# Moving weight splits, bank copies and the steps of a norm's root around the start of two feed-forward blocks

## The chip, the core and the metric

The program runs on one core of a Trainium2 chip. TensorE (PE) multiplies matrices and writes into PSUM, which has eight banks of 128 partitions by 512 fp32 numbers. VectorE (DVE) and ScalarE (ACT) do the work on elements, and SyncE (SP) issues nearly all the transfers. Each engine takes its own instructions in the order in which they stand and waits for the others on semaphores. The metric is the device time of one execution in microseconds (us); lower is better.

## The reference, cut to what matters

Two groups of tokens (512 and 256, held side by side as 768 columns) go through two layers. Each layer has a token mixer, a feed-forward block with squared ReLU, and a gated embedding that is added; a norm with its own gain stands ahead of each.

```python
def rms_norm(x, g):
    xf = x.astype(jnp.float32)
    y = xf * lax.rsqrt(jnp.mean(xf * xf, axis=-1, keepdims=True) + EPS)
    return (y * g.astype(jnp.float32)).astype(x.dtype)
...
        h = rms_norm(x, norm_mlp[i])
        x = x + jnp.square(jax.nn.relu(h @ mlp_w_up[i])) @ mlp_w_down[i]
        gate = jax.nn.sigmoid(rms_norm(x, norm_ple[i]) @ ple_w_gate[i])
        x = x + (p[i] @ ple_w_proj[i]) * gate
```

The model width is 1024, the width inside the feed-forward block is 4096, and everything is fp32.

## The kernel before

Features lie on the partitions and tokens along the free axis, so an activation of the whole model is eight tiles of 128x768. An fp32 product is made of three products of rounded parts: an operand is split into hi (ACT copies it with rounding) and lo (DVE subtracts hi from the source), and PE adds hi·hi, hi·lo and lo·hi. In a row, the split of a weight tile reads `whi<-wraw` or `zhi<-wraw` on ACT and `wlo` or `zlo` on DVE. The tiles of tag w have two buffers; those of tag z have one, so a `zhi` cannot be written before PE has read the last one for the last time.

A norm is applied late. The tiles that PE reads are x times the gain, without the root. The sum of squares `acc` is made beside it, split into `ah` and `al` (`acc_parts`), summed over partitions on PE with a matrix of ones (`ss`, four matmuls), and turned into the root in the three steps of `rstd_steps`: `logs` (a table load on ACT, `v` on DVE from both halves of ss, `ln` on ACT, each half behind its v, then `y` = exp), `newton` (a square on ACT, again called `ln`, and a new `v` on DVE), and `result` (the root `rstd`, on DVE). Only the evacuation of a product (`rectified`, rows `y<-p,rstd_mlp`) needs the root.

The feed-forward block has 16 chunks of 256 hidden features. Chunks 0 and 1 are plain (`up_plain`): 96 matmuls of 128x384, eight blocks of the input times three parts times two halves of the output (p1, p2) times two halves of the tokens (sides). Their weights are two raw tiles, the "direct" one, split into zhi and zlo, and the "second" one, split into whi and wlo. Later chunks use Strassen's seven products, for which the input has to be combined: for each of four pairs of blocks, `norm.combine` makes two scaled copies on ACT (`q`, `q`), two sums on DVE, a rounded `t` on ACT, two more sums, a second `t`, and two subtractions on DVE. I call these eleven steps a combination. Work tiles such as `q`, `v`, `ln` and `y` take six buffers in turn, so the second q of the third combination takes the buffer that `v` holds until the root is made.

In the first layer (layer 0) `ahead` runs before the block: it multiplies the second half of the projected input embedding in four products of 12 matmuls (`pj`, two banks each), copies the banks out on ACT (`pjs`) and stores them by SP, and makes the norm's root and the first two combinations beside it. Chunk 0 then knows its root (`known`) and makes the third and fourth combination. In layer 1 the first two combinations are made earlier, in the product ahead, and chunk 0 does not know its root: it makes the sum of squares, the root and the last two combinations while it multiplies. There its 96 matmuls come in four groups of 36, 36, 12 and 12 (n = 0 to 3).

PSUM is divided by tags: A has four banks, B and C two each. Inside `manual_schedule` the order on PE, ACT and DVE is the order in which the code is written, so a call that stands later in the code stands later in the engine's queue. `weave` takes one step of each list in turn.

Of the kernel before, what the change touches and what calls it, by code (L numbers as in the profile page):

```python
# [47 lines left out]
def trunk_kernel(ctx: ExitStack, tc: tile.TileContext, a: dict, out: bass.AP):  # L48
# [67 lines left out]
    def both(name="mm", tag=None):  # L116

        return [t[:, :H] for t in fresh(name, 2, tag)]
# [52 lines left out]
    class Norm:  # L171
# [30 lines left out]

        aside = temp

        def acc_parts(self):
            ah, al = self.aside("ah", F32R), self.aside("al", F32R)
            self.last = split(ah, al, self.acc)
            return ah, al

        def sum_squares(self, psum, also=None, parts=None, tag=None):  # L210

# [22 lines left out]
        def rstd_steps(self, psum, ss=None):  # L234
            n = self.n
            if ss is None:
                ss = self.sum_squares(psum)
            v, ln, y = (self.aside(name) for name in ("v", "ln", "y"))

            def logs():  # L240
                with tc.issue_after(self.last):
                    act.preload_act_table_set(EXP_LN)
                for t, o, e in ss:
                    dve.tensor_scalar(v[:, o:e], t, 1.0 / D, EPS, ALU.mult, ALU.add)  # L244
                for t, o, e in ss:
                    act.activation(ln[:, o:e], t, AF.Ln, scale=1.0 / D, bias=eps[:])  # L246
                act.activation(y, ln, AF.Exp, scale=-0.5)  # L247


            def newton():  # L250
                act.activation(ln, y, AF.Square)  # L251
                dve.scalar_tensor_tensor(v, ln, -0.5, v, ALU.mult, ALU.mult)  # L252

            def result():
                if self.rplace is None:
                    self.r = stat.tile([P, n], F32, tag="rstd", name=f"rstd_{self.name}")[:]
                else:
                    self.r = slot(self.rplace, f"rstd_{self.name}", F32)[:, :n]
                dve.scalar_tensor_tensor(self.r, v, 1.5, y, ALU.add, ALU.mult)  # L259

            return [logs, newton, result]
# [564 lines left out]
    def weave(*chains):  # L826

        for steps in itertools.zip_longest(*chains):
            for step in steps:
                if step:  # L830
                    step()
# [20 lines left out]
    def second_inputs(places):  # L852


        part = [], []
        ws = []

        def behind(i):
            if i < 2:
                raw = fetch(a["p"][1, :, i, :])  # L860
                hi, lo = (slot(places[2 * i + p], "p1") for p in range(2))
                split(hi[:], lo[:], raw[:, :T])
                part[0].append(hi[:])
                part[1].append(lo[:])
            elif i == 3:
                ws.append(weight(a["proj"][1, 1], 2))
            elif i == 5:
                ws.append(up_chunk(0, 0))
            elif i == 7:
                ws[1].split("second")  # L870

        def product(m):
            ps = both("pj", "AB"[m % 2])
            group2(ps, terms_of(ws[0], part, col=m * P))
            return ps

        return behind, product, ws

    def ahead(norm, product, w, places):


        ps = []

        def copied(m):
            t = slot(places[m], "pjs", F32)
            for f, o, e in pieces(ps[m]):
                act.activation(t[:, o:e], f, AF.Copy)
            nc.sync.dma_start(pj[1][KB // 2 + m], t[:])

        for m in range(KB // 2):  # L890
            ps.append(product(m))
            if m == 0:
                w.split("direct")
                parts = norm.acc_parts()
            else:
                copied(m - 1)
            if m == 2:
                weave(norm.combine(0))
        ss = norm.sum_squares(psum, parts=parts, tag="C")
        copied(m)  # L900
        weave(norm.rstd_steps(psum, ss), norm.combine(1))
        return norm.r

    def mlp(l, norm, nxt, w, places, early, product=None):
# [3 lines left out]
        r = None  # L908
# [7 lines left out]
        def squared(t):  # L916
            act.activation(t[:], t[:], AF.Square)  # L917
# [30 lines left out]
        def up_plain(u, w, make, then):  # L948
# [7 lines left out]
            def rects(*which):  # L956
                for i, o in which:
                    rectified((y1, y2)[i], ps[i][o], H * o, H * o + H, ALU.max)
# [5 lines left out]
            for n, (i, ks, sides) in enumerate(order):  # L964
                for k in range(*ks):
                    m, h = PAIRED[k] % (KB // 2), PAIRED[k] // (KB // 2)
                    c = slice(P * m, P * m + P)
                    hi, lo = w.w[f"w{i + 1}{h + 1}"]
                    for j, (wt, part) in enumerate(((hi, 0), (hi, 1), (lo, 0))):
                        for o in sides:  # L970
                            pe.matmul(
                                ps[i][o],
                                lhsT=wt[:, c],
                                rhs=xs[f"x{h + 1}{1 + o}"][m][part],
                                start=k == 0 and j == 0,
                                stop=k == KB - 1 and j == 2,
                            )
                if n == 0:
                    v = make()
                    split2 = [lambda: v.split("second")] if v.plain else []  # L980
                    todo1 = norm.combine(todo.pop(0)) if todo else []
                    rest, pend[:] = pend[:4], pend[4:]
                    if not known:
                        parts = norm.acc_parts()
                    weave(rest, todo1, split2)
                elif n == 1:
                    sums = [] if v.plain else [v.sums32, v.sums14, lambda: v.split("direct")]
                    weave(norm.combine(todo.pop(0)) if todo else [], sums, pend)
                    pend.clear()
                    if not known:  # L990
                        ss = norm.sum_squares(psum, parts=parts, tag="C")
                elif n == 2:
                    weave([lambda: v.split("direct" if v.plain else "s32")], [] if known else norm.rstd_steps(psum, ss))
                    r = norm.r
                    if known:
                        y1, y2 = big("y1"), big("y2")
                        rects((0, 1), (1, 1))
                else:
                    if not known:
                        y1, y2 = big("y1"), big("y2")  # L1000
                        rects((0, 1), (1, 1))
                    rects((0, 0))
                    squared(y1)
                    rects((1, 0))
                    pend.extend(acts_of(u, y1, y2, y2))
            return v
# [299 lines left out]
    for i, m in enumerate(PAIRED):  # L1306
        if i == 1:
            w += [weight(a["w_o0"][3], 4)] * 2
        ps = both()
# [103 lines left out]
```

## Time and profile before

| what | value |
|---|---|
| median of 3 runs | 1717.86 us (1717.43 to 1718.11) |
| the profiled execution | 1720.3 us, of which the span from first to last instruction is 1718.5 us |
| granted TensorE clock over the span | 0.991 |
| busy in the span | PE 97%, DVE 78%, ACT 50% |
| start of layer 0's feed-forward block | pj products 308.6 to 321.2 us, chunk 0 from 321.95, chunk 1 from 344.5, third chunk from 363.5 |
| start of layer 1's feed-forward block | chunk 0 from 1148.2 us, chunk 1 from 1165.7, third chunk from 1182.5 |

All times in rows are counted from the start of the span. A row of the timeline gives the start, the time from the start of the first to the end of the last instruction that it merges, the engine, the line, the operation, out<-in, the shape, the count, and in brackets the idle time of the engine before it with what ended that. The profiled execution's own time is its span and 1.8 us around it.

### The profile page before, as it was taken

Reading aid. Unit: us, or ns where it says so; the run is one execution under the profiler, and the core shown is the slowest. Engines: PE = TensorE matmul, PEld = TensorE weight load, DVE = VectorE, ACT = ScalarE, POOL = GpSimd, SP = SyncE. Lnnn points to the kernel's source line nnn. Section 1 sums busy time; section 2 is a strip of 40 time slices with the busy share of each in tenths; the row PEclk is TensorE's granted clock in tenths of the full one; section 3 lists DMA queues with packets and bytes.
Section 4 is the critical chain, followed back from the end, with each engine's and each line's share of the span. In section 5 each row is a group of like instructions: output and inputs, shape, how many; then the busy total and the mean of one; then the engine's idle time right before and its main releaser. Section 6 shows DMA issues by size and latency. Waiting matters only on the chain. (4 is left out here: it accounts for less than half of the span.)

```text
span 1718.5 us, 24204 instructions
## 1 busy us (share of the span) xinstructions
PE 1675.4 (97%) x9542; PEld 1617.8 (94%) x9542; DVE 1346.7 (78%) x2207; ACT 860.1 (50%) x1370; POOL 2.0 (0%) x30
## 2 busy tenths in 40 slices
PE   8999999899999999999999999999999999999996
PEld 7887788899999999999999999999999999999986
DVE  6588888889999989977765444668989999999676
ACT  6367756754454455544541111445455545555454
POOL 0000000000000000000000000000000000000000
PEclk9999999999999999999999999999999999999998
DMA  8753322211222222222321111211222222222222
GB/s 258 192 138 115 104 80 80 74 59 65 74 74 73 70 71 71 74 83 81 110 71 62 62 62 62 74 62 43 73 72 72 74 72 76 63 73 86 74 89 96
DMA packets 47842, 144.59 MB, mean 84 GB/s; under 512 B 6080, under 2 KB 10688, under 8 KB 47728
## 3 DMA queue, kind: packets, MB, share of 16 engines
q1 hardware_dynamic: 45168, 139.89, 25.8%
q10 hardware_dynamic: 2560, 3.15, 0.7%
q8 instruction: 75, 1.23, 0.3%
q14 instruction: 39, 0.32, 0.1%
HBM read 123.10 MB, written 10.48 MB: 78 GB/s over the span
## 5 line engine op out<-in xcount | busy, mean ns | idle before, releaser
L83 ACT ACTIVATE whi<-wraw 128x1024 fp32r<-128x1024 f32 (+2 forms) x73 | 75.5, 1034 | 185.6 <-PE b L129 53.0
L409 ACT ACTIVATE whi<-sum 128x1024 fp32r<-128x1024 f32 x56 | 59.0, 1053 | 146.6 <-PE a L441 146.6
L917 ACT ACTIVATE y<-y 128x768 f32<-128x768 f32 x64 | 53.5, 840 | 141.2 <-DVE y L914 141.2
L441 PE MATMUL a<-act,whi 128*128 128x384 f32 x448 | 96.7, 337 | 0.0
L84 DVE TENSOR_TENSOR wlo<-wraw,whi 128x1024 fp32r<-128x1024 f32 (+2 forms) x73 | 87.0, 1192 | 10.5 <-ACT whi L83 10.2
L441 PE MATMUL a<-t,zhi 128*128 128x384 f32 x448 | 92.2, 337 | 1.9 <-ACT c L1023 1.9
L441 PE MATMUL b<-t,zhi 128*128 128x384 f32 x448 | 92.0, 337 | 0.0
L441 PE MATMUL a<-t,whi 128*128 128x384 f32 x448 | 91.9, 337 | 0.0
L441 PE MATMUL a<-xs,whi 128*128 128x384 f32 x448 | 87.6, 337 | 0.8 <-DVE y L1046 0.8
L1079 DVE TENSOR_TENSOR x<-x,a 128x384 f32<-128x384 f32 x112 | 60.8, 553 | 33.7 <-PE a L441 33.5
L138 PE MATMUL mm<-xs_mix,whi 128*128 128x512 f32 (+1 forms) x320 | 82.9, 342 | 0.0
L441 PEld LDWEIGHTS a<-t,zhi 128*128 128x128 f32 x448 | 79.2, 188 | 2.2 <-ACT c L1023 2.2
L441 PEld LDWEIGHTS a<-xs,whi 128*128 128x128 f32 x448 | 79.0, 188 | 1.2 <-DVE y L1046 1.2
L441 PEld LDWEIGHTS a<-act,whi 128*128 128x128 f32 x448 | 79.8, 188 | 0.0
L441 PEld LDWEIGHTS b<-t,zhi 128*128 128x128 f32 x448 | 79.5, 188 | 0.0
L441 PEld LDWEIGHTS a<-t,whi 128*128 128x128 f32 x448 | 79.0, 188 | 0.0
L420 DVE TENSOR_TENSOR wlo<-sum,whi 128x1024 fp32r<-128x1024 f32 x56 | 68.5, 1223 | 9.6 <-ACT whi L409 9.6
L420 DVE TENSOR_TENSOR wlo<-wraw,whi 128x1024 fp32r<-128x1024 f32 x60 | 73.2, 1220 | 0.4 <-ACT whi L409 0.4
L409 ACT ACTIVATE zhi<-sum 128x1024 fp32r<-128x1024 f32 x56 | 59.3, 1060 | 20.9 <-DVE sum L385 16.5
L420 DVE TENSOR_TENSOR zlo<-sum,zhi 128x1024 fp32r<-128x1024 f32 x56 | 68.2, 1217 | 1.9 <-ACT zhi L409 1.9
L409 ACT ACTIVATE whi<-wraw 128x1024 fp32r<-128x1024 f32 x60 | 63.2, 1054 | 11.0 <-PE C L441 6.3
L330 ACT ACTIVATE t<-y 128x768 fp32r<-128x768 f32 x56 | 47.2, 843 | 41.1 <-DVE y L321 30.8
(290 smaller groups left out, 4639.2 us busy)
## 6 DMA issues: line engine op xcount, KB each, us to landing
wraw<-in_up SPq DMA_DIRECT2D x64, 512.0 KB, 3.5
wraw<-in_down SPq DMA_DIRECT2D x64, 512.0 KB, 3.5
wraw<-in_w_in SPq DMA_DIRECT2D x24, 512.0 KB, 3.4
wraw<-in_gate SPq DMA_DIRECT2D x16, 512.0 KB, 3.5
pj<-pjs SPq DMA_DIRECT2D x16, 384.0 KB, 3.6
wraw<-in_w_q SPq DMA_DIRECT2D x8, 512.0 KB, 4.8
wraw<-in_w_out SPq DMA_DIRECT2D x8, 512.0 KB, 3.5
x_in<-in_x SPq DMA_DIRECT2D x8, 384.0 KB, 7.1
```

What stands on the lines that cost most here:

```text
L83: first = act.activation(hi, src, AF.Copy)
L84: dve.tensor_tensor(lo, src, hi.bitcast(F32), ALU.subtract)
L138: pe.matmul(ps[:, o:e], lhsT=w, rhs=x[:, o:e], start=i == 0 and j == 0, stop=i == n - 1 and j == 2,)
L330: act.activation(t[0][:], (self.q1, self.q2)[i][:], AF.Copy)
L409: act.activation(hi[:], src, AF.Copy)
L420: dve.tensor_tensor(lo[:], src, hi[:].bitcast(F32), ALU.subtract)
L441: pe.matmul(ps, lhsT=a, rhs=b, start=start and i == 0, stop=i == len(terms) - 1, skip_group_check=True)
L917: act.activation(t[:], t[:], AF.Square)
L1079: dve.tensor_tensor(t[:, o : o + H], t[:, o : o + H], f, op)
```

## The change

The diff does four things.

1. In `ahead` the four products of the projected inputs take banks A, B, C, A in place of A, B, A, B, and ss takes B in place of C. The copy of a product is written behind the next product, as before, but `acc_parts` has moved from product 0 to behind copy 0, so that copy 0 stands ahead of `ah` and all the others behind it. The direct split of chunk 0 is written ahead of the products.
2. The table load becomes a step of its own (`table`), written right behind `acc_parts`.
3. In `ahead`, `logs` now stands ahead of the second combination, and `newton` and `result` behind it. In `up_plain` of a chunk that does not know its root, ss goes from n = 1 to n = 0, `logs` to the start of n = 1, `newton` and `result` to its end, behind the last combination, and the early scaled copies of the third combination go behind `acc_parts`.
4. The "direct" split of chunk 1's weights goes from n = 2, behind both combinations, to n = 1 between them where the root is known (layer 0). Where it is not known (layer 1) it stays at n = 2, ahead of which the whole root now stands. There, at the end of chunk 0, the evacuation of one half goes behind the square of y1.

On ACT in layer 0, from `ah` to the second combination. Before:

```order
L83 ACTIVATE ah<-acc_mlp_3328 128x768
L887 ACTIVATE pjs<-pj 128x384 x4
L303 ACTIVATE q<-x,vec 128x768
L304 ACTIVATE q<-x,vec 128x768
L330 ACTIVATE t_3678<-q 128x768
L330 ACTIVATE t_3683<-q 128x768
L887 ACTIVATE pjs<-pj 128x384 x4
L303 ACTIVATE q<-x,vec 128x768
L304 ACTIVATE q<-x,vec 128x768
L242 ACT_TABLE_LOAD
```

and now:

```order
L895 ACTIVATE pjs<-pj 128x384 x2
L303 ACTIVATE xs_3600<-x,vec 128x768
L195 ACTIVATE sq<-x 128x768
L83 ACTIVATE ah<-acc_mlp_3328 128x768
L216 ACT_TABLE_LOAD
L895 ACTIVATE pjs<-pj 128x384 x2
L311 ACTIVATE q<-x,vec 128x768
L312 ACTIVATE q<-x,vec 128x768
L338 ACTIVATE t_3679<-q 128x768
L338 ACTIVATE t_3684<-q 128x768
L895 ACTIVATE pjs<-pj 128x384 x4
L254 ACTIVATE ln<-ss,eps 128x384 x2
```

Product 0's two copies have gone ahead of `ah`, the table load has come between `ah` and product 1's two, and `ln` follows the last copies with no combination and no load between.

On ACT in layer 0, from the third combination of chunk 0 to the evacuation (the t are the rounded sums of a combination). Before:

```order
L304 ACTIVATE q<-x,vec 128x768
L409 ACTIVATE whi<-wraw 128x1024
L330 ACTIVATE t_3787<-q 128x768
L330 ACTIVATE t_3792<-q 128x768
L303 ACTIVATE q<-x,vec 128x768
L304 ACTIVATE q<-x,vec 128x768
L330 ACTIVATE t_3827<-q 128x768
L330 ACTIVATE t_3832<-q 128x768
L409 ACTIVATE zhi<-wraw 128x1024
L917 ACTIVATE y_3865<-y_3865 128x768
```

and now:

```order
L312 ACTIVATE q<-x,vec 128x768
L417 ACTIVATE whi<-wraw 128x1024
L338 ACTIVATE t_3787<-q 128x768
L338 ACTIVATE t_3792<-q 128x768
L417 ACTIVATE zhi<-wraw 128x1024
L311 ACTIVATE q<-x,vec 128x768
L312 ACTIVATE q<-x,vec 128x768
L338 ACTIVATE t_3831<-q 128x768
L338 ACTIVATE t_3836<-q 128x768
L930 ACTIVATE y_3865<-y_3865 128x768
```

`zhi` of chunk 1 has moved ahead of the fourth combination.

On ACT in layer 1, from the end of the third combination's t (t_11038 before, t_11039 now). Before:

```order
L330 ACTIVATE t_11038<-q 128x768
L303 ACTIVATE q<-x,vec 128x768
L304 ACTIVATE q<-x,vec 128x768
L330 ACTIVATE t_11085<-q 128x768
L330 ACTIVATE t_11090<-q 128x768
L409 ACTIVATE zhi<-wraw 128x1024
L242 ACT_TABLE_LOAD
L246 ACTIVATE ln<-ss,eps 128x384 x2
L247 ACTIVATE y<-ln 128x768
L251 ACTIVATE ln<-y 128x768
```

and now:

```order
L338 ACTIVATE t_11039<-q 128x768
L254 ACTIVATE ln<-ss,eps 128x384 x2
L255 ACTIVATE y<-ln 128x768
L311 ACTIVATE q<-x,vec 128x768
L312 ACTIVATE q<-x,vec 128x768
L338 ACTIVATE t_11100<-q 128x768
L338 ACTIVATE t_11105<-q 128x768
L259 ACTIVATE ln<-y 128x768
L417 ACTIVATE zhi<-wraw 128x1024
```

Here `zhi` stands behind all of the root's work on ACT, ahead of which it stood; the table load has gone up to `ah`. On DVE `zlo` moved in the same way:

```order
L260 SCALAR_TENSOR_TENSOR v<-ln,v 128x768
L267 SCALAR_TENSOR_TENSOR rstd_mlp_11112<-v,y 128x768
L428 TENSOR_TENSOR zlo<-wraw,zhi 128x1024
L927 SCALAR_TENSOR_TENSOR y_11142<-p_10976,rstd_mlp_11112 128x384
L927 SCALAR_TENSOR_TENSOR y_11142<-p_10975,rstd_mlp_11112 128x384
```

Before, `zlo<-wraw,zhi` stood ahead of the four v, rstd and evacuation rows there; now it stands behind the root.

```diff
--- before.py
+++ after.py
@@ -202,10 +202,19 @@
 
         aside = temp
 
+        ready = False
+
         def acc_parts(self):
             ah, al = self.aside("ah", F32R), self.aside("al", F32R)
             self.last = split(ah, al, self.acc)
             return ah, al
+
+        def table(self):
+
+            if not self.ready:
+                with tc.issue_after(self.last):
+                    act.preload_act_table_set(EXP_LN)
+            self.ready = True
 
         def sum_squares(self, psum, also=None, parts=None, tag=None):
 
@@ -238,8 +247,7 @@
             v, ln, y = (self.aside(name) for name in ("v", "ln", "y"))
 
             def logs():
-                with tc.issue_after(self.last):
-                    act.preload_act_table_set(EXP_LN)
+                self.table()
                 for t, o, e in ss:
                     dve.tensor_scalar(v[:, o:e], t, 1.0 / D, EPS, ALU.mult, ALU.add)
                 for t, o, e in ss:
@@ -870,7 +878,7 @@
                 ws[1].split("second")
 
         def product(m):
-            ps = both("pj", "AB"[m % 2])
+            ps = both("pj", "ABCA"[m])
             group2(ps, terms_of(ws[0], part, col=m * P))
             return ps
 
@@ -887,18 +895,23 @@
                 act.activation(t[:, o:e], f, AF.Copy)
             nc.sync.dma_start(pj[1][KB // 2 + m], t[:])
 
+        w.split("direct")
         for m in range(KB // 2):
             ps.append(product(m))
-            if m == 0:
-                w.split("direct")
+            if m > 0:
+                copied(m - 1)
+            if m == 1:
                 parts = norm.acc_parts()
-            else:
-                copied(m - 1)
-            if m == 2:
+                norm.table()
+            elif m == 2:
                 weave(norm.combine(0))
-        ss = norm.sum_squares(psum, parts=parts, tag="C")
+        ss = norm.sum_squares(psum, parts=parts, tag="B")
         copied(m)
-        weave(norm.rstd_steps(psum, ss), norm.combine(1))
+        logs, newton, result = norm.rstd_steps(psum, ss)
+        logs()
+        weave(norm.combine(1))
+        newton()
+        result()
         return norm.r
 
     def mlp(l, norm, nxt, w, places, early, product=None):
@@ -978,29 +991,41 @@
                 if n == 0:
                     v = make()
                     split2 = [lambda: v.split("second")] if v.plain else []
-                    todo1 = norm.combine(todo.pop(0)) if todo else []
                     rest, pend[:] = pend[:4], pend[4:]
                     if not known:
                         parts = norm.acc_parts()
-                    weave(rest, todo1, split2)
+                        norm.table()
+                    weave(rest, norm.combine(todo.pop(0)) if todo else [], split2)
+                    if not known:
+                        ss = norm.sum_squares(psum, parts=parts, tag="C")
                 elif n == 1:
+                    steps = [] if known else norm.rstd_steps(psum, ss)
+                    for step in steps[:1]:
+                        step()
+                    if known and v.plain:
+                        v.split("direct")
                     sums = [] if v.plain else [v.sums32, v.sums14, lambda: v.split("direct")]
                     weave(norm.combine(todo.pop(0)) if todo else [], sums, pend)
                     pend.clear()
-                    if not known:
-                        ss = norm.sum_squares(psum, parts=parts, tag="C")
+                    for step in steps[1:]:
+                        step()
+                    r = norm.r
                 elif n == 2:
-                    weave([lambda: v.split("direct" if v.plain else "s32")], [] if known else norm.rstd_steps(psum, ss))
-                    r = norm.r
+                    if not v.plain:
+                        v.split("s32")
+                    elif not known:
+                        v.split("direct")
                     if known:
                         y1, y2 = big("y1"), big("y2")
                         rects((0, 1), (1, 1))
                 else:
                     if not known:
                         y1, y2 = big("y1"), big("y2")
-                        rects((0, 1), (1, 1))
+                        rects((0, 1))
                     rects((0, 0))
                     squared(y1)
+                    if not known:
+                        rects((1, 1))
                     rects((1, 0))
                     pend.extend(acts_of(u, y1, y2, y2))
             return v
```

## The prediction

> **What bounds the kernel now.** I read the page first, then PE's waits, then the order of time in the two stretches that the diff touches.
>
> ```profile
> span 1718.5 us, 24204 instructions
> PE 1675.4 (97%) x9542; PEld 1617.8 (94%) x9542; DVE 1346.7 (78%) x2207; ACT 860.1 (50%) x1370; POOL 2.0 (0%) x30
> ...
> PE p L971 <- ACT zhi L409: 5.6, 1, 5.6
> ...
> PE pj L129 <- ACT pjs L887: 2.3, 1, 2.3
> ```
>
> PE is the bound: 1675.4 of 1718.5 us. The change removes no matmul, so it can only win PE's waits, and two of the longest (us in total, times, longest) are at places it edits. Both are in layer 0:
>
> ```profile
> 314.56 0.51 PE L129 MATMUL pj<-p,wlo 128*128 128x384 f32 x2
> 317.35 1.71 PE L129 MATMUL pj<-p,whi 128*128 128x384 f32 x4 [2.28 <-ACT pjs L887]
> 321.25 0.33 PE L226 MATMUL ss<-ah,ones 128*128 128x384 f32 x1
> 321.95 0.51 PE L971 MATMUL p<-x,zhi 128*128 128x384 f32 x2
> 344.48 1.01 PE L971 MATMUL p<-x,zhi 128*128 128x384 f32 x2 [5.60 <-ACT zhi L409]
> 345.74 0.69 PE L971 MATMUL p<-x,zlo 128*128 128x384 f32 x1 [0.25 <-DVE zlo L420]
> 363.46 1.55 PE L441 MATMUL a<-xs,whi 128*128 128x384 f32 x8
> 381.29 0.61 PE L441 MATMUL b<-t,zlo 128*128 128x384 f32 x2 [0.21 <-DVE zlo L420]
> ```
>
> A matmul normally starts every 0.175 us (four take 0.86 with their tail). Product 3 of pj waits 2.28 us for a bank, and its 12 matmuls then take 3.90 us (317.35 to 321.25) in place of 2.1. Chunk 1 waits 5.60 us for zhi and 0.25 for zlo. The long times behind each wait are the clock:
>
> ```profile
> 317.70:321.10 3.40, 3.40 (x12) 3.37 (x12) 2.24 (x5) 2.46 (x3) 0.00 (x0) 0.51 0.88 309
> 345.00:348.30 3.30, 3.05 (x10) 2.56 (x9) 2.55 (x5) 1.18 (x2) 0.00 (x0) 0.50 0.46 125
> 1188.00:1191.40 3.40, 2.64 (x15) 2.65 (x16) 2.54 (x3) 3.40 (x7) 0.00 (x0) 1.00 0.00 0
> ```
>
> The column behind the five engines is the granted clock: half for some 3.4 us behind both waits, full behind layer 1's shorter one of 1.87 us.
>
> Layer 1 has the same chunks, and no wait at its chunk 1:
>
> ```profile
> 1152.18 0.85 ACT L83 ACTIVATE ah<-acc_mlp 128x768 fp32r<-128x768 f32 x1 [1.22 <-DVE acc_mlp L196]
> 1163.42 1.06 ACT L409 ACTIVATE zhi<-wraw 128x1024 fp32r<-128x1024 f32 x1 [0.83 <-PE p L971]
> 1166.05 0.34 PE L971 MATMUL p<-x,zlo 128*128 128x384 f32 x1
> 1182.53 1.57 PE L441 MATMUL a<-xs,whi 128*128 128x384 f32 x8
> 1188.76 1.67 PE L441 MATMUL a<-t,zhi 128*128 128x384 f32 x8 [1.87 <-ACT c L1023]
> 1203.78 0.62 PE L441 MATMUL b<-t,zlo 128*128 128x384 f32 x2 [0.35 <-DVE zlo L420]
> ```
>
> There zhi starts as soon as PE has read the old one (0.83 <-PE), 2.3 us before chunk 1 wants it. The change makes it stand behind the root.
>
> **Durations for the sums.** ACT and DVE in layer 0:
>
> ```profile
> 315.17 0.84 ACT L83 ACTIVATE ah<-acc_mlp 128x768 fp32r<-128x768 f32 x1 [1.26 <-DVE acc_mlp L196]
> 316.04 1.64 ACT L887 ACTIVATE pjs<-pj 128x384 f32<-128x384 f32 x4
> 317.54 0.96 ACT L303 ACTIVATE q<-x,vec 128x768 f32<-128x768 f32 x1
> 321.94 1.61 ACT L887 ACTIVATE pjs<-pj 128x384 f32<-128x384 f32 x4
> 325.23 1.28 ACT L242 ACT_TABLE_LOAD   x1
> 326.52 1.05 ACT L246 ACTIVATE ln<-ss,eps 128x384 f32<-128x384 f32 x2
> 327.61 0.85 ACT L247 ACTIVATE y<-ln 128x768 f32<-128x768 f32 x1
> 333.16 0.92 ACT L303 ACTIVATE q<-x,vec 128x768 f32<-128x768 f32 x1
> 333.99 0.92 ACT L304 ACTIVATE q<-x,vec 128x768 f32<-128x768 f32 x1
> 338.28 0.84 ACT L330 ACTIVATE t<-q 128x768 fp32r<-128x768 f32 x1 [1.68 <-DVE q L326]
> 339.03 0.92 ACT L303 ACTIVATE q<-x,vec 128x768 f32<-128x768 f32 x1
> 343.39 1.04 ACT L409 ACTIVATE zhi<-wraw 128x1024 fp32r<-128x1024 f32 x1
> ...
> 329.37 0.96 DVE L252 SCALAR_TENSOR_TENSOR v<-ln,v 128x768 f32<-128x768 f32 x1 [3.57 <-ACT ln L251]
> 330.36 0.96 DVE L259 SCALAR_TENSOR_TENSOR rstd_mlp<-v,y 128x768 f32<-128x768 f32 x1
> 338.10 2.01 DVE L336 TENSOR_TENSOR t<-q,t 128x768 fp32r<-128x768 f32 x2
> 344.46 1.23 DVE L420 TENSOR_TENSOR zlo<-wraw,zhi 128x1024 fp32r<-128x1024 f32 x1
> ```
>
> From these: a pair of copies 0.8; a combination on ACT 4.40 (317.54 to 321.94), with a weight split in it 5.87 (333.16 to 339.03); a table load 1.29; ln to y 1.09; a 768-wide step on ACT 0.75 (338.28 to 339.03); the two subtractions end 1.83 behind the second t; v to root 0.99, the root 0.96; zlo 1.07 behind zhi; PE's first zlo matmul 1.28 behind the start of zlo.
>
> **Layer 0.** *Banks.* Product 3 has a free bank and ends at 314.90+2.1 = 317.0. Now ss needs bank pair B, so product 1's copies. ah is at 315.17 as before; behind it now comes the table load, to 317.3; product 1's copies end at about 317.85 and 318.25. So PE waits 0.85 us, ss takes its four matmuls, and chunk 0 starts at 318.6 in place of 321.95: 3.35 us earlier, with no slow stretch. The load ahead of the copies costs 1.28 of what the free bank wins. SP now has the first store ahead of chunk 1's second weight tile; the store's source is ready first, so nothing waits for it.
>
> *Chunk 1's weights.* ACT goes on: first combination from 318.1 to 322.5, four copies to 324.1, ln, y at 325.2, second combination from 326.0 to 330.4, ln to 331.2; DVE then makes v and the root by 333.2. The third combination's second q takes v's buffer, so it starts at 333.2, not at 331.95. From there as before (333.99 to 339.03, 5.04): zhi at 338.3, zlo at 339.35, the first zlo matmul at 340.6, against 345.74. Chunk 0 takes 16.8 us and ends at 335.4, so PE still waits 3.95 us for zhi and 0.9 for zlo: the wait shrinks, and the clock probably drops again.
>
> *What is late next.* That 5.1 us is not kept:
>
> ```profile
> 345.61 1.95 DVE L914 SCALAR_TENSOR_TENSOR y<-p,rstd_mlp 128x384 f32<-128x384 f32 x4
> 360.42 1.22 DVE L420 TENSOR_TENSOR zlo<-sum,zhi 128x1024 fp32r<-128x1024 f32 x1 [1.92 <-ACT zhi L409]
> 365.75 0.47 ACT L1023 ACTIVATE c<-a 128x384 f32<-128x384 f32 x1 [0.88 <-PE a L441]
> ```
>
> The fourth combination now follows zlo, and chunk 0's evacuation starts only some 1.05 us earlier. From it on ACT and DVE run their queues with two pauses that depend on PE: 1.92 us (zhi of sums waits until PE has read the z tile) and 0.88 us (the copy c waits for a). Both vanish, so c comes 1.05+1.92+0.88 = 3.85 us earlier, at 361.9, and PE, which wants it 4.2 us into the third chunk (361.1 at full clock, 362.4 at half), waits up to 1.2. DVE goes on without a pause for PE to the zlo of 381.29, which PE waited for already. So layer 0 is worth **-3.85 us**, whether the clock dropped in chunk 1 or not. Bounds: -5.1 if ACT and DVE catch up, -3.0 if 0.88 does not come back.
>
> **Layer 1.** ss moves ahead of group 1: al is ready 1.85 us behind ah's start (1154.0), PE is there at 1154.5, so it costs nothing; if al came 0.5 later it would cost what is above that. ACT now: ah 1152.18, table load to 1154.35, third combination with the split whi, whose second t is at 1154.35+5.87-0.75 = 1159.5; DVE's subtractions end at 1161.3, then v, so ln starts at 1161.8 and y at 1162.9; fourth combination from 1163.65 to 1168.05; ln; zhi at 1168.8, ready 1169.85. On DVE the subtractions end at 1169.1, v and root take until 1170.9, then zlo; its first matmul is at 1172.2, against 1166.05: **+6.1 us** (PE waits 4.1 for zhi, then 1.95 for zlo). That is layer 0's old stall, moved here. It brings the slow clock: chunk 1 from its first zlo matmul to the third chunk took 17.72 us in layer 0 (345.74 to 363.46) and 16.48 in layer 1 (1166.05 to 1182.53), so **+1.24**; the upper end is 1.80, product 3's. In return ACT and DVE gain time: from the third chunk's start to `b<-t,zlo` layer 1 took 21.25 us (1182.53 to 1203.78), layer 0 behind its stall 17.83, so **-3.42**. Sum +3.9, from +2.7 (clock holds) to +4.5.
>
> The Trainium skill (ScalarE: Activation LUTs, What ACT_TABLE_LOAD costs) adds a drain of about 1380 ns to the load's 1283 ns. Here ln starts 0.01 us behind the load (325.23+1.28, 326.52), so the row decides; by that page my sum would be an estimated 1.4 us worse, at 1719.3.
>
> **Sum.** -3.85 + 3.9 = +0.05 us. Against the profiled execution's 1720.3 that is 1720.35; the median of the runs shown, 1717.86, lies 2.4 below it, and the difference carries over: **1717.9 us**, no change. The likeliest case's own range is 1716.2 to 1719.6 (the ends of the two terms, rarely together).
>
> **The rivals.**
> *The clock holds in layer 1.* Then +2.7 there, 1716.7. For it: 1.87 us of waiting left the clock full. Against: 2.28 did not, and this stall is 4.1 and then 1.95. The Trainium skill (TensorE: Matmul & The Clock Gate, What's actually happening) lets the clock drop only behind a whole idle window of about 3.4 us, free-running; by it 2.28 us could not have halved the clock, and the row says it did; a stall of 4.1 would fill a window only in some positions, which is this rival.
> *Faster: layer 1's stall stays small.* If zhi were ready soon enough that layer 1 is neutral, layer 0's -3.85 stands alone: 1714.0. It decides once zhi starts before about 1165.2, which needs ACT 3.6 us ahead of my queue; the order of the rows speaks against it.
> *Slower: short waits drop the clock in layer 0's third chunk.* PE's new waits there (up to 1.2 for c, others of the kind behind it) are no longer hidden; each slow stretch costs up to 1.8. With two, 1721.5. It decides from two on; 1.87 us at 1188.76 left the clock full, which speaks against it.
>
> **How the numbers follow.** The sum as forecast 0.56, clock holds 0.16, faster 0.13, slower 0.15. About 0.2% (3.4 us) is what a measurement can tell from no change: faster than 1714.4 holds most of the third case (0.10), slower than 1721.3 most of the fourth (0.12), the rest is 0.78. Range for 8 in 10: 1715.0 to 1720.8, which leaves out most of the third and fourth case.
>
> **What would show it.** Right: chunk 0 of layer 0 at about 318.6, its chunk 1 waiting 4 us for zhi in place of 5.6, a short wait at `a<-t,zhi` there; in layer 1 a new wait of about 4 us for zhi at 1165.7, 2 for zlo, a clock of 0.5 behind it, and the waits of 1.87 and 0.35 gone or smaller. Wrong: no such wait in layer 1, or layer 0's third chunk coming 5 us earlier and staying so.

## The result: no change that can be told, and two changes of 4 to 6 us inside it

The changed kernel took 1718.44 us (median of 12 runs), the kernel before 1717.67 (12 runs): ratio 1.0004, 95% interval 0.9995 to 1.0013, which is +0.7 us with -0.9 to +2.2. The forecast was 1717.9. The profiled execution is 1719.2 us long, with a span of 1717.4.

The chain of the argument is in PE's waits. First the summary of the waits of the changed kernel (us in total, times, longest):

```profile
PE p L984 <- ACT zhi L417: 7.7, 2, 4.0
...
PE p L984 <- DVE zlo L428: 1.6, 2, 1.3
```

The wait for zhi at chunk 1 now stands there twice, once in each layer; the bank wait of pj product 3 (2.3 us) and layer 1's wait for c (1.9) are gone. The timeline of PE in layer 0:

```profile
305.88 0.86 PE L129 MATMUL pj<-p,whi 128*128 128x384 f32 x4
...
315.16 0.44 PE L235 MATMUL ss<-ah,ones 128*128 128x384 f32 x1 [0.70 <-ACT pjs L895]
...
315.99 0.52 PE L984 MATMUL p<-x,zhi 128*128 128x384 f32 x2
...
336.69 1.01 PE L984 MATMUL p<-x,zhi 128*128 128x384 f32 x2 [3.75 <-ACT zhi L417]
337.95 0.69 PE L984 MATMUL p<-x,zlo 128*128 128x384 f32 x1 [0.25 <-DVE zlo L428]
...
356.41 1.55 PE L449 MATMUL a<-xs,whi 128*128 128x384 f32 x8
...
374.77 0.62 PE L449 MATMUL b<-t,zlo 128*128 128x384 f32 x2 [0.37 <-DVE zlo L428]
```

The first pj matmul starts 2.72 us earlier than in the profile before (308.60), although nothing ahead of it was changed. Where that comes from is told at the end; it means that the two profiles must be compared by distances inside a stretch. From the first pj matmul, chunk 0 now starts after 10.11 us (13.35 before), chunk 1's first zlo matmul after 32.07 (37.14), the third chunk after 50.53 (54.86), and the zlo of `b<-t,zlo` after 68.89 (72.69). So layer 0 won 3.24, then 5.07, then 4.33, and kept **3.80 us**. Nothing of it is lost later: from the first pj matmul to layer 1's chunk 0 it is 835.71 us (839.61 before).

Why 3.80 is kept of the 5.07 is seen on DVE and ACT:

```profile
342.06 1.94 DVE L927 SCALAR_TENSOR_TENSOR y<-p,rstd_mlp 128x384 f32<-128x384 f32 x4
354.87 1.22 DVE L428 TENSOR_TENSOR zlo<-sum,zhi 128x1024 fp32r<-128x1024 f32 x1
359.21 0.47 ACT L1048 ACTIVATE c<-a 128x384 f32<-128x384 f32 x1
```

From the first pj matmul, chunk 0's evacuation starts 0.83 us earlier than before, `zlo<-sum` 2.83 and c 3.82 us earlier. The two pauses of the profile before (1.92 and 0.88 us) are gone.

The timeline of PE in layer 1:

```profile
1141.59 0.34 PE L984 MATMUL p<-xs,zhi 128*128 128x384 f32 x1
...
1163.22 1.01 PE L984 MATMUL p<-x,zhi 128*128 128x384 f32 x2 [3.98 <-ACT zhi L417]
1165.53 0.69 PE L984 MATMUL p<-x,zlo 128*128 128x384 f32 x1 [1.30 <-DVE zlo L428]
...
1184.90 1.57 PE L449 MATMUL a<-xs,whi 128*128 128x384 f32 x8
...
1202.74 0.62 PE L449 MATMUL b<-t,zlo 128*128 128x384 f32 x2
```

From chunk 0's first matmul (1148.21 before), the first zlo matmul of chunk 1 comes after 23.94 us (17.84 before), the third chunk after 43.31 (34.32), the zlo of `b<-t,zlo` after 61.15 (55.57). Layer 1 lost 6.10 us at the stall, 2.89 more inside chunk 1, and got 3.41 back in the third chunk: **+5.58 us**. What PE waited for there is seen in the timelines of ACT and DVE:

```profile
1155.19 1.05 ACT L254 ACTIVATE ln<-ss,eps 128x384 f32<-128x384 f32 x2 [1.49 <-DVE v L252]
...
1161.40 0.83 ACT L259 ACTIVATE ln<-y 128x768 f32<-128x768 f32 x1
1162.13 1.04 ACT L417 ACTIVATE zhi<-wraw 128x1024 fp32r<-128x1024 f32 x1
```

```profile
1163.38 0.96 DVE L267 SCALAR_TENSOR_TENSOR rstd_mlp<-v,y 128x768 f32<-128x768 f32 x1
1164.26 1.22 DVE L428 TENSOR_TENSOR zlo<-wraw,zhi 128x1024 fp32r<-128x1024 f32 x1
```

zhi follows the last ACT step of the root, and zlo the root itself on DVE. Layer 0's old stall has moved to layer 1.

The 2.89 us are the clock. The windows of 3.41 us around the stall (the columns behind the times: busy time of PE, PEld, DVE, ACT and POOL, the granted clock, then DMA's share and GB/s):

```profile
1158.05:1161.46 3.41, 1.19 (x7) 0.87 (x5) 3.04 (x5) 2.38 (x4) 0.00 (x0) 1.00 0.00 0
1161.46:1164.87 3.41, 1.01 (x2) 0.50 (x2) 3.31 (x4) 1.71 (x3) 0.00 (x0) 0.50 0.00 0
1164.87:1168.29 3.42, 2.76 (x9) 2.76 (x10) 2.47 (x5) 1.76 (x3) 0.00 (x0) 0.50 0.47 139
1168.29:1171.70 3.41, 3.41 (x12) 3.41 (x11) 2.79 (x5) 1.32 (x3) 0.00 (x0) 0.50 0.04 14
1171.70:1175.11 3.41, 3.41 (x21) 3.41 (x21) 3.34 (x7) 2.40 (x3) 0.00 (x0) 1.00 0.00 0
```

The clock was half in three windows, 10.24 us. The wait for zlo reached into the second of them, which was followed by a third at half; only behind a window in which PE was busy throughout did the clock come back. From zhi on, PE multiplied at half clock for 8.5 us (1163.22 to 1171.70). 6.2 us of that lie behind the first zlo matmul (1165.53); at half speed they lose an estimated 3.1 us, close to the 2.89. Behind layer 0's stall before, which I had taken the price from, that was less than 4 us (344.48 to 348.3).

### The profile page after: what moved, and what is told of

The parts are those of the page before. It is cut to its first block, busy times and chain, and to the rows that moved or that the text cites. A ratio compares the mean times of both kernels' runs of the same rounds, so it can differ in the third digit from the quotient of the medians.

```text
span 1717.4 us, 24206 instructions
## 1 busy us (share of the span) xinstructions
PE 1675.5 (98%) x9542; PEld 1618.0 (94%) x9542; DVE 1346.4 (78%) x2207; ACT 859.9 (50%) x1370; POOL 2.0 (0%) x30
## 4 chain that ended last, share of the span: by engine, by line
PE 66%; DVE 24%; ACT 7%; issue 2%; DMA 0%; DVEq 0%; ACTq 0%; SPq 0%
PE a L449 13%; PE mm L129 9%; PE mm L138 8%; PE gate L129 4%; PE b L129 4%; PE c L129 4%; PE u L129 4%; PE C L449 3%; PE B L449 3%; PE b L449 3%; DVE t L344 3%; DVE wlo L428 3%; DVE y L927 3%; PE gate L138 3%; DVE zlo L428 2%
```

## The experiments

My theory: layer 0 gains and layer 1 loses, and the two cancel. The rivals: neither moved the time; or layer 0's gain lies elsewhere than I put it. The eight runs below came in two sets of four, each set on one chip beside the kernel before (median 1718.44 us of 27 runs, then 1717.48 of 21). The table puts the trace beside the time: "layer 0" is the change of the distance from the first pj matmul to the zlo of `b<-t,zlo`, "layer 1" that from chunk 0's first matmul to the same place there, both in us against the profile before (72.69 and 55.57).

| kernel | layer 0 | layer 1 | sum | ratio of times (95%) | that is, us |
|---|---|---|---|---|---|
| the change | -3.80 | +5.58 | +1.78 | 1.0004 (0.9995 to 1.0013) | +0.7 |
| layer 0 only | -3.80 | 0.00 | -3.80 | 0.9969 (0.9960 to 0.9978) | -5.3 |
| layer 1 only | +0.12 | +5.46 | +5.58 | 1.0027 (1.0018 to 1.0036) | +4.6 |
| banks, copies, root only | +0.18 | -0.02 | +0.16 | 0.9997 (0.9988 to 1.0005) | -0.5 |
| split only, 5 runs | -3.09 | -0.01 | -3.10 | 0.9964 (0.9952 to 0.9977) | -6.2 |
| split only, 11 runs | -3.10 | 0.00 | -3.10 | 0.9984 (0.9975 to 0.9992) | -2.7 |
| the change, layer 1's zhi early | -3.83 | +0.74 | -3.09 | 0.9982 (0.9973 to 0.9990) | -3.1 |
| both mended | -4.96 | -2.17 | -7.13 | 0.9960 (0.9946 to 0.9973) | -6.9 |
| both mended, zhi in the third | -5.29 | -2.18 | -7.47 | 0.9952 (0.9940 to 0.9965) | -8.2 |

**Layer 0 alone.** In `up_plain`, the chunk that does not know its root is put back in the old order:

```diff
-                        norm.table()
...
-                    if not known:
-                        ss = norm.sum_squares(psum, parts=parts, tag="C")
                 elif n == 1:
-                    steps = [] if known else norm.rstd_steps(psum, ss)
-                    for step in steps[:1]:
-                        step()
...
+                    if not known:
+                        ss = norm.sum_squares(psum, parts=parts, tag="C")
                 elif n == 2:
+                    here = [] if known and v.plain else [lambda: v.split("direct" if v.plain else "s32")]
+                    weave(here, [] if known else norm.rstd_steps(psum, ss))
```

> Layer 0 as in the changed kernel, the first chunks of layer 1 in the order of the kernel before. My theory (a gain in layer 0 and a loss in layer 1 that cancel): the loss goes and layer 0's -3.85 us stands alone, about 1713.8 us against 1717.7, ratio 0.9978. Rival (neither layer moved the time, and the two profiles differ by chance): within 1 us of the kernel before, ratio 0.9994 to 1.0006. In the profile: the wait for zhi at layer 1's chunk 1 is gone, and the wait for c in its third chunk, 1.87 us before, is back.

Measured: ratio 0.9969 (0.9960 to 0.9978), and no wait at layer 1's chunk 1. The wait for c is back, at the old size, and in this execution half the clock follows it (the row behind it is of the view by windows):

```profile
1179.25 1.95 PE L449 MATMUL a<-t,zhi 128*128 128x384 f32 x8 [1.87 <-ACT c L1039]
```

```profile
1180.43:1183.85 3.42, 3.42 (x12) 3.42 (x11) 3.21 (x6) 2.70 (x5) 0.00 (x0) 0.50 0.00 0
```

That costs nothing: the wait of 0.84 us for y that came some 9.5 us later in the profile before is gone in its place, and layer 1's distance is the same (55.57).

The rival "neither moved" falls. The forecast ratio, 0.9978, lies at the edge of the interval; the trace has the expected 3.80 us.

**Layer 1 alone.** The reverse: `ahead` of the kernel before, layer 0's split back behind both combinations, the new order only where the root is not known.

```diff
                 elif n == 1:
                     steps = [] if known else norm.rstd_steps(psum, ss)
                     for step in steps[:1]:
                         step()
-                    if known and v.plain:
-                        v.split("direct")
...
                 elif n == 2:
-                    if not v.plain:
-                        v.split("s32")
-                    elif not known:
-                        v.split("direct")
+                    v.split("direct" if v.plain else "s32")
```

> Only layer 1's chunk 0 in the new order, layer 0 as in the kernel before. My theory: slower by what the prediction gave layer 1, 3.9 us (1721.6, ratio 1.0023), or by 5.5 us (1723.2, ratio 1.0032) if the half clock behind the stall lasts as long as in the profile of the changed kernel (8.5 us). Rival (neither layer moved the time): within 1 us of 1717.7. In the profile: a wait of about 4 us for zhi at layer 1's chunk 1 and 1.3 to 1.9 for zlo behind it.

Measured: ratio 1.0027 (1.0018 to 1.0036), slower by 4.6 us. Both of my figures, 3.9 and 5.5, lie in the interval; the trace, with +5.46, has the second:

```profile
1168.03 1.01 PE L979 MATMUL p<-x,zhi 128*128 128x384 f32 x2 [3.99 <-ACT zhi L417]
1170.34 0.69 PE L979 MATMUL p<-x,zlo 128*128 128x384 f32 x1 [1.30 <-DVE zlo L428]
```

and again three windows at half clock, the first of them beginning inside the wait:

```profile
1166.00:1176.24 10.24, 6.91 (x20) 6.40 (x21) 8.56 (x13) 4.81 (x7) 0.00 (x0) 0.50 0.15 51
```

So the change is the sum of its two layers: -3.80 and +5.5 in the traces, -5.3 and +4.6 in the times, against +0.7 measured for both.

**Layer 0's two parts.** First the banks, copies, table load and root order of `ahead` without the move of the split. Against the kernel of layer 0 alone:

```diff
-                    if known and v.plain:
-                        v.split("direct")
...
                 elif n == 2:
-                    here = [] if known and v.plain else [lambda: v.split("direct" if v.plain else "s32")]
-                    weave(here, [] if known else norm.rstd_steps(psum, ss))
+                    weave([lambda: v.split("direct" if v.plain else "s32")], [] if known else norm.rstd_steps(psum, ss))
```

> Only the banks, copies, table load and root of layer 0 in the new order; chunk 1's weight split stays behind the fourth combination, layer 1 as before. My theory: chunk 0 starts 3.3 us earlier, but zhi of chunk 1 only 0.75 us earlier, so PE waits 8 us there in place of 5.6, and the time falls by about 0.8 us (1716.9, ratio 0.9995). Rival (the bank wait and its slow clock are the gain of layer 0): 3.3 us, 1714.4, ratio 0.9981.

Measured: 0.9997 (0.9988 to 1.0005). The rival's 0.9981 is outside. Chunk 0 starts 3.24 us earlier, and all of it is waited away at chunk 1:

```profile
341.15 1.01 PE L984 MATMUL p<-x,zhi 128*128 128x384 f32 x2 [8.12 <-ACT zhi L417]
342.41 0.69 PE L984 MATMUL p<-x,zlo 128*128 128x384 f32 x1 [0.25 <-DVE zlo L428]
...
361.02 1.55 PE L449 MATMUL a<-xs,whi 128*128 128x384 f32 x8
```

zhi did come 0.70 us earlier, as expected (0.75), but chunk 1 then took 18.61 us in place of 17.72, since the clock was half for three windows (336.83 to 347.07) and 5.9 us of them lay behind the longer wait, in place of 3.9 before. A wait with its slow clock that goes from PE, 4.1 us lost at product 3 (2.28 of waiting and 1.8 by the slow clock), was worth nothing while the next wait was for an engine that had its own queue to finish.

Then the split alone, on the kernel before:

```diff
                 elif n == 1:
+                    if known and v.plain:
+                        v.split("direct")
```

(and nothing for it at n = 2)

> Only the move of chunk 1's weight split between the third and fourth combination of layer 0; banks, copies, root and layer 1 as before. My theory: zhi of chunk 1 starts at 339.0 in place of 343.4, chunk 1's first zlo matmul comes 4.3 us earlier, and behind it ACT's and DVE's two pauses (1.92 and 0.88 us) go, so 2.8 us of it stay: 1714.9, ratio 0.9984. Rival (the bank wait is the gain of layer 0): under 0.6 us, ratio above 0.9996. In both the wait of 2.28 us at pj product 3 stays.

Measured in 5 runs: 0.9964 (0.9952 to 0.9977), 6.2 us, which neither theory had. The trace has 3.09 between the two marks, so I ran the same kernel again.

> The kernel with only layer 0's weight split moved, once more with more runs, since its 5 runs gave 0.9964 (-6.1 us) where 2.8 was expected and its trace has 3.1 between the first pj product and the b<-t,zlo of the third chunk. My theory: the trace's 3.1 us is the effect and the rest was the position of the clock's windows in those few runs, ratio 0.998 to 0.9985. Rival (the split alone is worth 6 us, more than with the banks moved): 0.9964 again.

Measured in 11 runs: 0.9984 (0.9975 to 0.9992), 2.7 us. The expected 2.8 lies in this interval and not in that of the first 5 runs; the traces have 3.1 both times. The granted clock points to a part of the difference: its mean over the runs was 0.994 for those 5 against 0.992 for the kernel before beside them, then 0.9934 against 0.9925. A thousandth of the clock is 1.7 us of the span, so that is an estimated 1.9 of the 3.5 us between the two results; the rest stays open. The two profiles of this one kernel show something else, side by side. In the first the clock fell at the wait for zhi, and chunk 1 took 18.80 us from its first zlo matmul (335.55):

```profile
334.29 1.01 PE L979 MATMUL p<-x,zhi 128*128 128x384 f32 x2 [2.71 <-ACT zhi L417]
...
354.35 1.55 PE L449 MATMUL a<-xs,whi 128*128 128x384 f32 x8
```

In the second it did not, chunk 1 took 16.54 us, and PE waited in the third chunk instead:

```profile
337.43 0.62 PE L979 MATMUL p<-x,zhi 128*128 128x384 f32 x2 [1.17 <-ACT zhi L417]
338.69 0.45 PE L979 MATMUL p<-x,zlo 128*128 128x384 f32 x1 [0.64 <-DVE zlo L428]
...
355.23 1.55 PE L449 MATMUL a<-xs,whi 128*128 128x384 f32 x8
...
360.49 1.67 PE L449 MATMUL a<-t,zhi 128*128 128x384 f32 x8 [0.90 <-ACT c L1034]
...
369.99 1.68 PE L449 MATMUL a<-xs,whi 128*128 128x384 f32 x8 [0.86 <-DVE y L1057]
```

From the first pj matmul to the zlo of `b<-t,zlo` both took 69.6 us. That is what the prediction meant by layer 0 being worth the same "whether the clock dropped in chunk 1 or not": ACT's and DVE's queue sets the third chunk.

**Layer 1 with zhi ahead of the fourth combination.** The changed kernel with its rule for layer 0 used in both layers:

```diff
-                    if known and v.plain:
+                    if v.plain:
                         v.split("direct")
...
-                    elif not known:
-                        v.split("direct")
```

> The changed kernel with one edit: in layer 1 too, chunk 1's weight split stands behind the logs and ahead of the fourth combination; the early table load, ss and logs of layer 1 stay. My theory (layer 1 loses only because zhi stands behind the root): no wait of 4 us at its chunk 1 and no half clock behind it, so layer 1 comes back to within 0.5 us of the kernel before, and the waits for c in its third chunk return; the time falls to that of the run with layer 0 alone or 0.5 us above it, 1713 to 1715, ratio 0.997 to 0.998. Rival (the new order of the root itself costs layer 1 its time): as the changed kernel, ratio 1.000 to 1.001.

Measured: 0.9982 (0.9973 to 0.9990). That is just above my 0.997 to 0.998, and the rival's 1.000 to 1.001 is outside. The stall is gone, layer 1 is 0.74 us slower than before where I had allowed 0.5, and the wait for c is back, longer, with a half window behind it:

```profile
1181.35 2.93 PE L449 MATMUL a<-t,zhi 128*128 128x384 f32 x8 [2.56 <-ACT c L1046]
```

The root's new order costs little by itself; where zhi stands costs the other 4.84 of the 5.58 us. The order gains nothing either. That what DVE and ACT have to do ahead of c is the same would explain it, but no run shows that by itself.

**A version that beats both.** Since c and its like are set by DVE's queue, what helps is to take away the pauses in which DVE waits for ACT. In layer 0 the table load goes behind product 1's copies, and the second combination is begun (its two copies) ahead of the logs. In layer 1 the table load stays behind `ah` and ss behind the first group, the fourth combination is begun ahead of the logs, and zhi stands ahead of newton. The third combination is begun ahead of `acc_parts`, and the last rectified half stands as in the kernel before. Against the changed kernel:

```diff
             if m == 1:
                 parts = norm.acc_parts()
-                norm.table()
             elif m == 2:
+                norm.table()
                 weave(norm.combine(0))
...
+        second = norm.combine(1)
         logs()
-        weave(norm.combine(1))
+        weave(second)
...
+                    todo1 = norm.combine(todo.pop(0)) if todo else []
...
-                    weave(rest, norm.combine(todo.pop(0)) if todo else [], split2)
+                    weave(rest, todo1, split2)
...
-                    steps = [] if known else norm.rstd_steps(psum, ss)
-                    for step in steps[:1]:
-                        step()
+                    todo2 = []
+                    if not known:
+                        steps = norm.rstd_steps(psum, ss)
+                        todo2 = norm.combine(todo.pop(0))
+                        steps[0]()
...
-                    weave(norm.combine(todo.pop(0)) if todo else [], sums, pend)
+                    weave(todo2 or (norm.combine(todo.pop(0)) if todo else []), sums, pend)
...
+                    here = [] if known and v.plain else [lambda: v.split("direct" if v.plain else "s32")]
+                    weave(here, [] if known else steps[1:])
```

> A version meant to beat both. Layer 0 as in the changed kernel, but the table load behind product 1's copies, and the second combination's two copies ahead of ln. Layer 1: table load behind ah and ss behind the first group as in the changed kernel; the fourth combination's two copies, then the logs, then the rest of that combination, then zhi, and newton and the root behind it. My theory, from rows: ss no longer waits 0.70; in layer 0 DVE no longer waits 2.36 us for the second combination's copies, so zhi of chunk 1 comes 1.05 us earlier and all behind it too (-4.9 in place of -3.85); in layer 1 zhi comes 0.9 us late for chunk 1 with the clock full, and DVE gains the table load's 1.28 and about 1 us of waits, so the third chunk's waits (1.87, 0.84) nearly go, -2.3. Sum -7.2: ratio 0.9958. Rival (what is won ahead of the third chunk waits there again): as with layer 0 alone, 0.997.

Measured: 0.9960 (0.9946 to 0.9973), 1710.13 us of 5 runs, against 0.9958 expected; layer 0 -4.96 and layer 1 -2.17 in the trace, against -4.9 and -2.3. The gain in layer 1 is seen in ACT's and DVE's timelines:

```profile
1152.99 1.03 ACT L254 ACTIVATE ln<-ss,eps 128x384 f32<-128x384 f32 x2
...
1156.27 1.05 ACT L417 ACTIVATE zhi<-wraw 128x1024 fp32r<-128x1024 f32 x1
```

```profile
1158.54 0.95 DVE L260 SCALAR_TENSOR_TENSOR v<-ln,v 128x768 f32<-128x768 f32 x1
1159.53 0.96 DVE L267 SCALAR_TENSOR_TENSOR rstd_mlp<-v,y 128x768 f32<-128x768 f32 x1
```

ACT does the logs while DVE works on the combination, and DVE's v no longer pauses for ACT. zlo costs PE 0.69 us at chunk 1, and of the third chunk's waits only one of 0.31 is left. How much each of these edits won by itself was not measured.

Last, the same with layer 0's chunk-1 split woven into the third combination:

```diff
-                    weave(rest, todo1, split2)
+                    direct0 = [lambda: None, lambda: None, lambda: None, lambda: v.split("direct")] if known and v.plain else []
+                    weave(direct0, rest, todo1, split2)
...
-                    if known and v.plain:
-                        v.split("direct")
```

> As the run before this one, but layer 0's chunk 1 split is woven into the third combination, ahead of its second t, some 2.5 us earlier. My theory (behind chunk 1 ACT and DVE work through a queue that sets the third chunk, whatever PE does before): PE's wait at chunk 1 falls from about 3.8 to 1.3 us with 1.4 us for zlo behind it, and the time falls by no more than 0.3 us against the run before. Rival (PE's wait at chunk 1 is what layer 0 still loses): 2.4 us less than the run before, or more where the half clock behind the wait goes with it.

Measured: 0.9952 (0.9940 to 0.9965), 1709.46 us of 5 runs. PE's waits moved:

```profile
332.85 0.62 PE L985 MATMUL p<-x,zhi 128*128 128x384 f32 x2 [0.89 <-ACT zhi L417]
334.63 0.45 PE L985 MATMUL p<-x,zlo 128*128 128x384 f32 x1 [1.16 <-DVE zlo L428]
...
358.15 1.67 PE L449 MATMUL a<-t,zhi 128*128 128x384 f32 x8 [2.62 <-ACT c L1045]
...
367.65 1.65 PE L449 MATMUL a<-xs,whi 128*128 128x384 f32 x8 [0.86 <-DVE y L1068]
```

Chunk 1's wait for zhi fell from 3.43 to 0.89 us and its clock stayed full, so the third chunk came 4.52 us sooner; 4.19 us were lost again in that chunk, most of them to the waits for c and y shown here. In the trace 0.33 is left of it, as my theory had it, and from the first pj matmul to layer 1's chunk 0 it is 0.31 (834.25 us against 834.56). By the times the two versions (0.9960 and 0.9952) can't be told apart, and the rival's 2.4 us isn't excluded by them; the two traces speak against it.

## The prediction, point by point

**Layer 0, right, and in its steps.** Chunk 0 was forecast 3.35 us earlier and came 3.24; the wait of 0.85 for the bank of ss was 0.70; chunk 1's wait for zhi was forecast at 3.95 and was 3.75 (the 0.9 for zlo behind it was 0.25, since the two matmuls between took 1.01 us at half clock); its first zlo matmul came 5.07 us earlier, forecast 5.14 (340.6 against 345.74). Forecast to stay: 3.85; stayed: 3.80. The step on which this rests, that ACT's and DVE's queue sets the third chunk, came as told: both pauses went, and c came 3.82 us earlier (3.85 forecast). The evacuation's own part was 0.83 in place of 1.05, which the rest of the queue made up. One step was different in this execution: the wait of up to 1.2 us for c did not appear, since 5.6 us of the half clock lay behind the wait at chunk 1 in place of 3.9, and PE came to the third chunk later. In the second run of the split alone, where the clock held, the wait was there (0.90). The separate runs show that the banks alone are worth about nothing (-0.5 us by time, 0.18 the other way in layer 0's trace). By the traces most of the 3.80 is the split (3.10), and the banks add 0.7 once the split is moved; the times are too wide to tell these 0.7.

**Layer 1, right in kind, one term too small.** The stall: forecast 4.1 and 1.95 us of waiting and 6.1 us in all; 3.98, 1.30 and 6.10 measured. The gain in the third chunk: forecast 3.42, measured 3.41. The step that failed is the price of the slow clock behind the stall, +1.24 with an upper end of 1.80: it was 2.89, and 2.77 in the run of layer 1 alone. I had taken the price from stalls in which the half clock outlasted the wait by 3.9 us (chunk 1 of layer 0) and 3.7 us (product 3). Here the second wait, for zlo, fell into the half-clock stretch and was followed by another window at half. With 2.89 the layer's sum is +5.58, beyond the +4.5 that I gave as its upper end.

**The sum.** +0.05 forecast, +1.78 by the trace, +0.7 with -0.9 to +2.2 by time. That it came out so near owes something to the width of the measurement: the missing 1.73 us lies within it.

**The rivals.** That the clock holds in layer 1: no, in neither of two traces with this stall. Other executions may have been luckier: of the 11 runs of layer 1 alone, two have a granted clock of 0.992 over the span and took 1718.74 and 1719.01 us, while the other nine have 0.988 or 0.989 and took 1720.88 to 1725.85 us. Three half windows are an estimated 0.003 of the clock, so in those two the clock may have held here; neither has a trace that shows it. That layer 1's stall stays small: no here; with zhi ahead of the fourth combination it did, and the time went to 0.9982, near the 1714.0 which that rival gave. That short waits in layer 0's third chunk drop the clock: in the profiles with such waits (0.86 with layer 0 alone, 0.90 and 0.86 with the split, 2.62 and 0.86 in the last) the clock stayed full there. But the evidence that I gave against it, 1.87 us of waiting that left the clock full, was one execution's; the last section shows others in which it did not. The point of the Trainium skill (ScalarE: Activation LUTs, What ACT_TABLE_LOAD costs) on a drain of about 1380 ns beside a table load is not borne out by the rows: in the changed kernel the load takes 1.28 us from 313.32, 0.02 us behind `ah`, and ACT's next instruction starts 0.01 us behind its end. The time can't tell 1.4 us.

## What to carry to other kernels

Before a wait of the bound engine is priced, follow the engine it waits for to the end of its queue: a wait that goes away (here 4.1 us at the banks) is worth only what that engine, too, reaches earlier. When a helper's order is changed at every place that calls it, look at each place apart: the root's steps, moved forward, were harmless in layer 0, but in layer 1 zhi came to stand behind the root and cost what layer 0 had won. To win (6.9 us here), fill the pauses of the engine that sets the next wait (begin a combination ahead of the logs), rather than move a wait along.

## What the runs showed of the hardware

*The clock depends on where its windows lie.* The granted clock falls and rises on a grid of about 3.41 us: the stretches at half clock were 3.41, 6.83 or 10.24 us long, but for the one at the end of each execution. The place of the grid against the program differed from execution to execution, and with it which waits cost. Between 155 and 218 us, where no kernel here differs, the profile before had three such windows and that with layer 0 alone none:

```profile
155.00:218.00 63.00, 56.95 (x296) 45.51 (x295) 48.30 (x149) 44.27 (x113) 0.00 (x0) 0.92 0.45 135
```

```profile
155.00:218.00 63.00, 55.80 (x315) 44.97 (x315) 51.65 (x153) 44.06 (x114) 0.00 (x0) 1.00 0.47 140
```

(the first row is the kernel before, the second layer 0 alone). The first pj matmul started at 308.60 and 302.95 us in the two. Three windows at half clock cost some 3 x 1.7 = 5.1 us of work, which is most of that difference and as much as either layer's effect; the 27 runs of the kernel before in one comparison lay between 1715.51 and 1720.87 us. A single pair of profiles would have been read wrongly by their spans.

*Neither the length of a wait nor PE's busy time decides it.* Product 3's wait for its bank was 2.28 us in both profiles of the kernel with the split alone. In the first the clock stayed full, and product 3 took 2.43 us from its first matmul to ss:

```profile
311.51 1.18 PE L129 MATMUL pj<-p,whi 128*128 128x384 f32 x4 [2.28 <-ACT pjs L895]
...
313.94 0.34 PE L235 MATMUL ss<-ah,ones 128*128 128x384 f32 x1
```

In the second a half window began at 316.23, and product 3 took 3.10 us (3.90 in the profile before). In the same way layer 1's wait for c, 1.87 us with the clock full in the profile before, was followed by a half window in the four other profiles that have it at that length (1.86 or 1.87: layer 0 only, banks only, both of the split alone). So the 1.87 and the 2.28 between which the prediction looked for the clock's step were each what one execution had.

The Trainium skill (TensorE: Matmul & The Clock Gate, What's actually happening) has the clock drop behind a whole idle window of a free-running grid. The grid is what the traces show, the whole idle window is not. These are two windows, each with the one behind it, first of layer 1 alone, then of the changed kernel with layer 1's zhi early:

```profile
210.27:213.68 3.41, 2.24 (x11) 1.08 (x9) 3.40 (x11) 2.31 (x4) 0.00 (x0) 1.00 0.80 241
213.68:217.09 3.41, 3.05 (x8) 2.22 (x8) 3.38 (x6) 2.66 (x10) 0.00 (x0) 0.50 0.97 273
```

```profile
160.55:163.96 3.41, 1.67 (x11) 1.23 (x9) 1.45 (x4) 2.82 (x11) 0.00 (x0) 1.00 0.83 269
163.96:167.38 3.42, 3.30 (x21) 2.84 (x22) 2.28 (x7) 2.53 (x6) 0.00 (x0) 1.00 0.49 170
```

Behind the first, in which PE was busy 2.24 of 3.41 us, the clock was half; behind the second, busy 1.67, it stayed full. What the throttle counts stays open; in these windows PE's busy time in the profile is not it.
